# A hand-written stage order changed at three places, and the feed-forward transposes moved behind the per-layer projection

## The chip, the cores and the metric

The kernel runs on one core of a Trainium2 chip. The metric is the device time of one execution in microseconds (us). The engines are TensorE (PE, with PEld for its weight loads), VectorE (DVE), ScalarE (ACT), GpSimd (POOL) and SyncE (SP), which issues the DMA transfers.

## The reference

Two encoder layers are computed in float32 on x of 256 positions by 1024 channels. Cut to what matters here:

```python
h = rms_norm(x, g_mix)
proj = h @ w_in               # latents c_q, c_kv, k_r; d_q, d_k, d_v; s_q, s_k, s_v; gates
q = (rms_norm(c_q, g_q_lora) @ w_uq)     # latent attention "mla": rotary part from sin, cos
kv = (rms_norm(c_kv, g_kv_lora) @ w_ukv)
o_mla, o_diff, o_win = ...    # three attentions; the last two subtract slope * |distance|
merged = (gates[:, :, 0] * (o_mla @ w_branch[0]) + gates[:, :, 1] * (o_diff @ w_branch[1])
          + gates[:, :, 2] * (o_win @ w_branch[2]))
x = x + merged @ w_out
h = rms_norm(x, g_ffn)
x = x + (gelu(depthwise_conv(h @ w_ffn_gate)) * (h @ w_ffn_up)) @ w_ffn_down
e = rms_norm(pe @ w_ple_proj, g_ple)
return x + sigmoid(rms_norm(x, g_ple_in) @ w_ple_gate) * e
```

## The kernel before

Every product is made from three TensorE matmuls: each float32 operand is split into a high part (fp32r) and the low rest, and hi·hi, hi·lo and lo·hi are summed in PSUM. Weights come through the class `Stream` (`W`) in blocks of 128 x 1024 numbers: SP loads `raw` (L80), ACT copies it to `whi` (L91), and DVE subtracts to `wlo` (L92). Each of the three has four buffers; loads run four blocks ahead of use and splits two. Activations are turned by TensorE transposes (`TR`, L330) into PSUM banks and split there in the same way by `split` (L347: ACT at L349 or L352, DVE at L350 or L353). PSUM has four banks for transposes, scores and small outputs (`bank`) and four accumulators (`accbank`).

Of one layer, in the order of time: the projection "A" of the latents; then the mixers, whose stages stand in the string `ORDER` (L51 to L57), one word for a stage or for one weight block of a projection; then the output projection (`out1`), the per-layer projection of pe (`pp0`, `pp1`), the normalised x (`xn`), its transposes `ffnT`, and the feed-forward part in 11 steps of gate (`g`), up (`u`) and down blocks.

Words of `ORDER` that matter: `g01`, `g11`, `g20`, `g21` are units of gate projections (one weight block, 12 matmuls); `ukv0`, `uq0`, `uq1` the second latent projections; `Tmk0`, `Tmq0` transpose the normed keys (`uk00tok`, `uk01tok`) and queries (`uq00tok`, `uq01tok`) of the latent attention into banks `mk0b`, `mq0b`; `dq` is a projection for the differential attention; `dt3` transposes its last head (`od3` into `dot`) for the branch product `b10`; `ws1` are window scores (`w1s`), `wo0` and `wo3` window outputs (`w0o`, `w3o`); `b20` is the window's branch product.

What a key tile needs: POOL computes mean squares and inverse roots (`uk00ms`, `uk00ri` at L730 and L732, and the same for `uq`), and `positions_setup` (L269) makes angles, sine and cosine and the mask of distances once for both layers (DVE L277 to L310, ACT L304, POOL L311 and L313); POOL multiplies sine and cosine into rotary factors `rpq`, `rpk` (L256 to L259), DVE rotates the shared key (`kr`, `krr`, L424 to L427), POOL scales it (L550), and DVE writes both parts of `uk00tok` (L795, L796).

The Python order is only a first list. A scheduler of the framework orders each engine's instructions from it, by priorities; an engine then runs its own list strictly in order. `tc.high_priority(offset=HI)` moves work up in that choice. So the change of one place can move instructions of other engines.

Of the kernel before, what the change touches and what calls it, by code (L numbers as in the profile page):

```python
# [18 lines left out]
P = 128  # L19
D = 1024  # L20
S = 256
DEPTH = 2
KT = D // P
NT = S // P
# [11 lines left out]
HI = 400  # L36
# [3 lines left out]
R_CW, R_CB, R_MIX, R_FFN, R_PIN, R_QL, R_KL = 0, 66, 88, 96, 104, 112, 114  # L40
# [8 lines left out]


ORDER = """  # L51
g00 g00 cT g00 g00 g01 ukv0 uq0 g01 g01 Tmk0 g01 Tmq0 uq1 dq ukv1 dq dq dq ms0 Tmk1 ms1 dk Tmq1 mp0 dk dk mp1
dk Tdq dv ms2 mo0 ms3 dv mp2 dv Tdk mp3 dv sq ms4 mo1 ms5 sq sq mp4 sq mp5 ms6 skv mo2 mp6 skv ms7 mp7 ds0 mo3
b00 Tsq Tskv b00 dp0 ds1 b01 b01 do0 g10 ds2 g10 dp1 do1 g10 dt0 ds3 g10 dp2 g11 dt1 do2 dp3 ws0 g11 g11 do3
g11 dt2 wp0 dt3 b10 ws1 wo0 b10 ws2 b11 b11 g20 wp1 ws3 g20 wp2 g20 wo1 g20 wo2 wp3 wo3 b20 b20 g21 g21 g21
Tmg0 g21 b21 b21
"""  # L57

# [59 lines left out]
def kernel(ctx: ExitStack, tc: tile.TileContext, a: dict, out: bass.AP):  # L118
# [23 lines left out]
    def bank(name):  # L142
        return psm.tile([P, 512], F32, tag="ps", name=name)
# [8 lines left out]
    ident = const.tile([P, P], F32, name="ident")  # L152
# [173 lines left out]
    def MM(*args, **kw):  # L326
        last_pe[0] = nc.tensor.matmul(*args, **kw)  # L327

    def TR(o, i, idn):
        last_pe[0] = nc.tensor.transpose(o, i, idn)  # L330
# [16 lines left out]
    def split(hi, lo, src, scale=None):  # L347
        if scale is None:
            ih = nc.scalar.activation(hi, src, AF.Copy)  # L349
            il = nc.vector.tensor_tensor(lo, src, hi.bitcast(F32), op=ALU.subtract)  # L350
        else:
            ih = nc.scalar.activation(hi, src, AF.Copy, scale=scale)  # L352
            il = nc.vector.scalar_tensor_tensor(lo, src, scale, hi.bitcast(F32), op0=ALU.mult, op1=ALU.subtract)  # L353
        return ih, il
# [20 lines left out]
            res.append(ri)  # L375
        return res

    def transpose_half(src, h, hi, lo, gcol, name, scale=None, k_base=None):
        res = []
        for kp in range(2):  # L380
            b = bank(f"{name}T{h}{kp}")
            bv = b.rearrange("p (a n) -> p a n", a=2)
            for i in range(2):
                c = (kp * 2 + i) * P
                for t in range(NT):
                    TR(bv[:, i, t * P:(t + 1) * P], src[t][h][:, c:c + P], ident)
            k0 = (h * 4 if k_base is None else k_base) + kp * 2
            if gcol is None:
                res.append(split(hi[:, k0:k0 + 2, :], lo[:, k0:k0 + 2, :], bv, scale))
            else:  # L390
                for i in range(2):
                    res.append(split(hi[:, k0 + i, :], lo[:, k0 + i, :], bv[:, i, :], gcol(k0 + i)))
        return res

    def gemm(name, nk, n, lhs, evict, alloc=None):
# [99 lines left out]
    def layer(l):  # L495
        n_ = f"L{l}"
        g = G[l]
# [90 lines left out]
        gT = g["T"]  # L588
# [411 lines left out]
        def T_mg(h):  # L1000
            if not mlT:
                mlT["h"] = big.tile([P, KT, S], F32R, tag="big", name=n_ + "mTh")
                mlT["l"] = big.tile([P, KT, S], F32R, tag="big", name=n_ + "mTl")
            transpose_half(mg["m"], h, mlT["h"], mlT["l"], None, n_ + "mg", 0.5)
# [13 lines left out]
        for tok in PLAN:  # L1018
            op = tok[0]
            if op == "f":  # L1020
                c = tok[1]
# [38 lines left out]
        b = bank(n_ + "peT").rearrange("p (a n) -> p a n", a=2)  # L1060
# [10 lines left out]
        xn = [[xnt[:, t, h, :] for h in range(2)] for t in range(NT)]  # L1071
# [25 lines left out]
            yield from gemm(f"{n_}pp{h}", 2, 512, lhs_p, evict_e(h))  # L1097
        fT = [big.tile([P, KT // 2, 2, S], F32R, tag="big", name=f"{n_}fT{h}") for h in range(2)]
        for h in range(2):
            with tc.high_priority(offset=HI):  # L1100
                transpose_half(xn, h, fT[h][:, :, 0, :], fT[h][:, :, 1, :],
                               lambda k, h=h: gT[:, R_FFN + 4 * h + k:R_FFN + 4 * h + k + 1], n_ + "ffn", k_base=0)

        def finish_e():
            for f in late_e:
                f()
            for t in range(NT):
                s1 = small(1, f"{n_}se{t}")
                nc.gpsimd.tensor_tensor(s1, sse[t][:, 0:1], sse[t][:, 1:2], op=ALU.add)
                r = rsqrt_mean(s1, D, 1, f"{n_}e{t}")  # L1110
                rh = sm.tile([P, 1], F32, tag="reh", bufs=2, name=f"{n_}reh{t}")
                nc.gpsimd.tensor_scalar(rh, r, 0.5, None, op0=ALU.mult)
                nc.vector.tensor_scalar(e_t[:, t, :], e_t[:, t, :], rh, None, op0=ALU.mult)
# [9 lines left out]
        def down(s):  # L1123
            hh, hl = hid.pop(s)
            for i in range(2):
                wh, wl = W.get()
                first, last = s == 0 and i == 0, s == NF // 2 - 1 and i == 1
                th = [(t, h) for h in range(2) for t in range(NT)]
                if last:
                    steps = [(m, t, h) for t, h in th for m in range(3)]  # L1130
                else:
                    steps = [(m, t, h) for m in range(3) for t, h in th]
                for m, t, h in steps:
                    MM(dacc[t][h], (hl if m == 2 else hh)[:, i, t * P:(t + 1) * P],
                       (wl if m == 1 else wh)[:, 0, h * 512:(h + 1) * 512], start=first and m == 0, stop=last and m == 2)

        for s in range(NF // 2):
            pb = {}
            for nm in ("g", "u"):
                bs = [bank(f"{n_}{nm}{s}{i}") for i in range(2)]  # L1140
                ws = [W.get(), W.get()]
                for i in range(2):
                    c = slice(i * P, (i + 1) * P)
                    for k in range(KT):
                        wh, wl = ws[k // 4]
                        xp = fT[k // 4][:, k % 4]
                        MM(bs[i], wh[:, k % 4, c], xp.rearrange("p a n -> p (a n)"), start=k == 0, stop=False)
                        MM(bs[i][:, :S], wl[:, k % 4, c], xp[:, 0, :], start=False, stop=k == KT - 1)
                pb[nm] = tmp.tile([P, 2, S], F32, tag="p" if nm == "g" else "t512", bufs=5 if nm == "g" else 3, name=f"{n_}{nm}s{s}")
                for i in range(2):  # L1150
                    o = pb[nm][:, i, :]
                    nc.scalar.activation(o, bs[i][:, S:], AF.Copy)
                    nc.vector.tensor_tensor(o, bs[i][:, :S], o, op=ALU.add)  # L1153
                if s == 0 and nm == "g":
                    finish_e()
            c = tmp.tile([P, 2, S], F32, tag="p", name=f"{n_}c{s}")
            for i in range(2):
                ff = s * 2 + i

                def tap(j):  # L1160
                    r = R_CW + j * NF + ff
                    return gT[:, r:r + 1]

                nc.scalar.activation(c[:, i, :], pb["g"][:, i, :], AF.Identity, scale=tap(1), bias=gT[:, R_CB + ff:R_CB + ff + 1])  # L1164
                nc.vector.scalar_tensor_tensor(c[:, i, 1:S], pb["g"][:, i, 0:S - 1], tap(0), c[:, i, 1:S], op0=ALU.mult, op1=ALU.add)
                nc.vector.scalar_tensor_tensor(c[:, i, 0:S - 1], pb["g"][:, i, 1:S], tap(2), c[:, i, 0:S - 1], op0=ALU.mult, op1=ALU.add)
            cf = c.rearrange("p a n -> p (a n)")
            sq = tmp.tile([P, 512], F32, tag="t512", bufs=3, name=f"{n_}c2{s}")
            nc.scalar.activation(sq, cf, AF.Square)
            nc.vector.scalar_tensor_tensor(sq, sq, 1.0 / GELU_A, cf, op0=ALU.add, op1=ALU.mult)  # L1170
            th = tmp.tile([P, 512], F32, tag="p", name=f"{n_}th{s}")
            nc.scalar.activation(th, sq, AF.Tanh, scale=GELU_C * GELU_A)
            nc.vector.scalar_tensor_tensor(th, th, 1.0, cf, op0=ALU.add, op1=ALU.mult)
            hd = th
            nc.vector.tensor_tensor(hd, th, pb["u"].rearrange("p a n -> p (a n)"), op=ALU.mult)
            hh = ptp.tile([P, NT, S], F32R, tag="pthi", name=f"{n_}hh{s}")
            hl = ptp.tile([P, NT, S], F32R, tag="ptlo", name=f"{n_}hl{s}")
            split(hh, hl, hd.rearrange("p (a n) -> p a n", a=2), 0.5)
            hid[s] = (hh, hl)
            if s:  # L1180
                down(s - 1)
            yield
# [53 lines left out]
    for l in range(DEPTH):  # L1236
        for _ in layer(l):
            pass
# [24 lines left out]
```

## Time and profile before

| what | value |
|---|---|
| median of 3 runs | 931.65 us (931.29 to 932.65) |
| profiled execution | 933.81 us, of which its span is 931.9 us |
| mean granted TensorE clock | 0.997 |
| busy shares of the span | PE 98%, PEld 82%, DVE 78%, ACT 68%, POOL 13% |
| DMA | 155.9 MB, 167 GB/s mean |

The profiled execution is 2.16 us over the median, 0.23%; 1.9 us of it lie outside the span. A busy share counts overlapping matmuls once, and the granted clock of 1.00 is TensorE's 2.4 GHz, 0.50 its 1.2 GHz.

### The profile page before, as it was taken

How to read it: one execution, taken by the hardware profiler on the slowest of the kernel's cores; microseconds unless marked ns; L12 is line 12 of the kernel's file. 1: busy time of each engine (PE TensorE's matmuls, PEld its weight loads, DVE VectorE, ACT ScalarE, POOL GpSimd, SP SyncE). 2: the span in 40 equal slices, each digit the busy share in tenths (PEclk: the TensorE clock that was granted, in tenths of full speed). 3: DMA queues.
4: the chain of work that ended last, by engine and by line, in shares of the span. 5: the costliest groups of instructions: out<-in, count | busy, mean ns of one | idle time of the engine just before them, and what ended most of it. 6: DMA issues, size and time to landing. Idle time of an engine off the chain costs nothing.

```text
span 931.9 us, 13773 instructions
## 1 busy us (share of the span) xinstructions
PE 912.8 (98%) x4807; PEld 767.2 (82%) x4807; DVE 728.6 (78%) x1281; ACT 632.9 (68%) x1172; POOL 125.3 (13%) x239
## 2 busy tenths in 40 slices
PE   7999999999999999999999999999999999999997
PEld 6878887788888888888888888787887888888886
DVE  4788789887688877778777887989767877877784
ACT  5868877884567566566676788688755766656572
POOL 2834021000020000000134423000001100000010
PEclk9999999999999999999999999999999999999999
DMA  6656435355546556666556555344464565556642
GB/s 194 210 154 199 137 103 158 114 157 187 185 129 210 190 182 194 194 185 186 161 149 185 178 158 155 105 149 125 127 217 157 170 211 181 185 183 194 195 150 88
DMA packets 101706, 155.90 MB, mean 167 GB/s; under 512 B 7316, under 2 KB 58372, under 8 KB 101636
## 3 DMA queue, kind: packets, MB, share of 16 engines
q1 hardware_dynamic: 101636, 155.02, 53.7%
q8 instruction: 38, 0.62, 0.3%
q14 instruction: 32, 0.26, 0.1%
HBM read 153.95 MB, written 1.05 MB: 166 GB/s over the span
## 4 chain that ended last, share of the span: by engine, by line
PE 87%; POOL 3%; DVE 3%; ACT 2%; issue 2%; DMA 1%; SPq 1%; POOLq 0%; ACTq 0%; DVEq 0%
PE L1u L327 7%; PE L0u L327 7%; PE L1g L327 7%; PE L0g L327 7%; PE L1dn L327 6%; PE L0dn L327 6%; PE L0g20a L327 1%; PE L1g20a L327 1%; PE L0dva L327 1%; PE L1dva L327 1%; PE L1g00a L327 1%; PE L1dka L327 1%; PE L0dka L327 1%; PE L0pg0a L327 1%; PE L1g21a L327 1%
## 5 line engine op out<-in xcount | busy, mean ns | idle before, releaser
L92 DVE TENSOR_TENSOR wlo<-raw,whi 128x1024 fp32r<-128x1024 f32 (+3 forms) x292 | 350.5, 1205 | 90.6 <-ACT whi L91 89.7
L91 ACT ACTIVATE whi<-raw 128x1024 fp32r<-128x1024 f32 (+3 forms) x292 | 304.0, 1044 | 135.2 <-PE L0dn L327 13.1
L327 PE MATMUL L0u<-L0fT,whi 128*128 128x512 f32 x176 | 62.7, 398 | 0.0
L327 PE MATMUL L1u<-L1fT,whi 128*128 128x512 f32 x176 | 62.7, 398 | 0.0
L327 PE MATMUL L1g<-L1fT,whi 128*128 128x512 f32 x176 | 62.5, 398 | 0.0
L327 PE MATMUL L0g<-L0fT,whi 128*128 128x512 f32 x176 | 62.5, 398 | 0.0
L327 PE MATMUL L1u<-L1fT,wlo 128*128 128x256 f32 x176 | 49.4, 281 | 0.0
L327 PE MATMUL L0u<-L0fT,wlo 128*128 128x256 f32 x176 | 49.4, 281 | 0.0
L327 PE MATMUL L0g<-L0fT,wlo 128*128 128x256 f32 x176 | 49.2, 281 | 0.0
L327 PE MATMUL L1g<-L1fT,wlo 128*128 128x256 f32 x176 | 49.2, 281 | 0.0
L327 PEld LDWEIGHTS L1u<-L1fT,whi 128*128 128x128 f32 x176 | 33.1, 188 | 8.3
L327 PEld LDWEIGHTS L0u<-L0fT,whi 128*128 128x128 f32 x176 | 33.1, 188 | 8.2
L327 PEld LDWEIGHTS L1g<-L1fT,whi 128*128 128x128 f32 x176 | 33.0, 188 | 8.0
L327 PEld LDWEIGHTS L0g<-L0fT,whi 128*128 128x128 f32 x176 | 33.0, 188 | 8.0
L327 PEld LDWEIGHTS L1g<-L1fT,wlo 128*128 128x128 f32 x176 | 33.2, 189 | 0.5
L327 PEld LDWEIGHTS L0g<-L0fT,wlo 128*128 128x128 f32 x176 | 33.2, 189 | 0.5
L327 PEld LDWEIGHTS L0u<-L0fT,wlo 128*128 128x128 f32 x176 | 33.2, 189 | 0.0
L327 PEld LDWEIGHTS L1u<-L1fT,wlo 128*128 128x128 f32 x176 | 33.2, 189 | 0.0
L372 POOL TENSOR_SCALAR L1plem<-L1pless 128x1 f32<-128x1 f32 x2 | 1.5, 732 | 176.9 <-ACT L1plej L368 176.9
L372 POOL TENSOR_SCALAR L0plem<-L0pless 128x1 f32<-128x1 f32 x2 | 1.5, 728 | 176.9 <-ACT L0plej L368 176.9
L1164 ACT ACTIVATE L0c<-L0gs,gT 128x256 f32<-128x256 f32 x22 | 13.3, 603 | 17.3 <-DVE L0gs L1153 17.3
L1164 ACT ACTIVATE L1c<-L1gs,gT 128x256 f32<-128x256 f32 x22 | 13.3, 603 | 17.3 <-DVE L1gs L1153 17.3
(1732 smaller groups left out, 2564.7 us busy)
## 6 DMA issues: line engine op xcount, KB each, us to landing
raw<-in_w_in_dram SPq DMA_DIRECT2D x84, 512.0 KB
raw<-in_w_ffn_gate_dram SPq DMA_DIRECT2D x44, 512.0 KB
raw<-in_w_ffn_up_dram SPq DMA_DIRECT2D x44, 512.0 KB
raw<-in_w_ffn_down_dram SPq DMA_DIRECT2D x44, 512.0 KB
raw<-in_w_branch_dram SPq DMA_DIRECT2D x24, 512.0 KB
raw<-in_w_out_dram SPq DMA_DIRECT2D x16, 512.0 KB
raw<-in_w_ple_gate_dram SPq DMA_DIRECT2D x16, 512.0 KB
raw<-in_w_in_dram SPq DMA_DIRECT2D x8, 416.0 KB
```

The costliest lines, as they stand in the source:

```text
L91: ih = self.nc.scalar.activation(hi[:, :m], raw[:, :m], AF.Copy)
L92: il = self.nc.vector.tensor_tensor(lo[:, :m], raw[:, :m], hi[:, :m].bitcast(F32), op=ALU.subtract)
L327: last_pe[0] = nc.tensor.matmul(*args, **kw)
L372: nc.gpsimd.tensor_scalar(ms, ss[t][:, 0:1], ss[t][:, 1:2], EPS, op0=ALU.add, op1=ALU.add)
L1164: nc.scalar.activation(c[:, i, :], pb["g"][:, i, :], AF.Identity, scale=tap(1), bias=gT[:, R_CB + ff:R_CB + ff + 1])
```

## The change

Three groups of words in `ORDER` change places. `transpose_half` issues all its transposes first, alternates the banks from one 128-column block to the next where a gain is given per block (the transposes of normed x for the mixers, for the gate of the per-layer input and for the feed-forward part), and raises the priority only of the splits. In the feed-forward part the first gate step goes through its channel blocks in the outer loop, so that its two outputs alternate.

```diff
-g00 g00 cT g00 g00 g01 ukv0 uq0 g01 g01 Tmk0 g01 Tmq0 uq1 dq ukv1 dq dq dq ms0 Tmk1 ms1 dk Tmq1 mp0 dk dk mp1
+g00 g00 cT g00 g00 g01 ukv0 uq0 g01 g01 g01 Tmk0 uq1 Tmq0 dq ukv1 dq dq dq ms0 Tmk1 ms1 dk Tmq1 mp0 dk dk mp1
...
-g11 dt2 wp0 dt3 b10 ws1 wo0 b10 ws2 b11 b11 g20 wp1 ws3 g20 wp2 g20 wo1 g20 wo2 wp3 wo3 b20 b20 g21 g21 g21
+g11 dt2 wp0 b10 ws1 dt3 wo0 b10 ws2 b11 b11 g20 wp1 ws3 g20 wp2 g20 wo1 g20 wo2 wp3 b20 g21 wo3 b20 g21 g21
...
+        bs = [bank(f"{name}T{h}{e}").rearrange("p (a n) -> p a n", a=2) for e in range(banks)]
+        where = [(k // 2, k % 2) if gcol is None else (k % banks, k // banks) for k in range(4)]
+        for k, (e, i) in enumerate(where):
+            for t in range(NT):
+                TR(bs[e][:, i, t * P:(t + 1) * P], src[t][h][:, k * P:(k + 1) * P], ident)
+        with tc.high_priority(offset=prio):
...
+                for k, (e, i) in enumerate(where):
+                    res.append(split(hi[:, k0 + k, :], lo[:, k0 + k, :], bs[e][:, i, :], gcol(k0 + k)))
...
-            with tc.high_priority(offset=HI):
-                transpose_half(xn, h, fT[h][:, :, 0, :], fT[h][:, :, 1, :],
-                               lambda k, h=h: gT[:, R_FFN + 4 * h + k:R_FFN + 4 * h + k + 1], n_ + "ffn", k_base=0)
+            transpose_half(xn, h, fT[h][:, :, 0, :], fT[h][:, :, 1, :],
+                           lambda k, h=h: gT[:, R_FFN + 4 * h + k:R_FFN + 4 * h + k + 1], n_ + "ffn", k_base=0, prio=HI)
...
+                blocks = [(i, k) for i in range(2) for k in range(KT)]
+                if s == 0 and nm == "g":
+                    blocks.sort(key=lambda b: b[1])
```

What the scheduler makes of it is shown at three places. The first is DVE in layer 0, where the keys of the latent attention are finished; `kr`, `krr` are the shared rotary key, `uk..tok`, `uq..tok` the key and query tiles. Before:

```order
L761 TENSOR_REDUCE L0uq01ss<-L0uq01sq 128x4
L92 TENSOR_TENSOR wlo_671<-raw_596,whi_670 128x768
L795 TENSOR_TENSOR L0uk00tok<-L0ukv0a_557,L0uk00ri 128x4x64
L796 TENSOR_TENSOR L0uk00tok<-L0krr_420,L0uk00ri 128x4x32
L795 TENSOR_TENSOR L0uk01tok<-L0ukv0a_558,L0uk01ri 128x4x64
L796 TENSOR_TENSOR L0uk01tok<-L0krr_438,L0uk01ri 128x4x32
L766 TENSOR_TENSOR L0uq00tok<-L0uq0a_594,L0uq00ri 128x384
```

With the change (L795 and L796 of before are L798 and L799 there, L766 is L769):

```order
L769 TENSOR_TENSOR L0uq00tok<-L0uq0a_594,L0uq00ri 128x384
L92 TENSOR_TENSOR wlo_689<-raw_632,whi_688 128x1024
L305 TENSOR_SCALAR nsinT<-sinT 128x32
L92 TENSOR_TENSOR wlo_727<-raw_668,whi_726 128x512
L428 TENSOR_TENSOR L0kr_422<-L0araw_142,rpk_403 128x16
L428 TENSOR_TENSOR L0kr_440<-L0araw_143,rpk_403 128x16
L429 TENSOR_TENSOR L0kr_440<-L0araw_143,rpk_403 128x16
L430 TENSOR_TENSOR L0krr_420<-L0kr_421,L0kr_422 128x32
L769 TENSOR_TENSOR L0uq01tok<-L0uq0a_595,L0uq01ri 128x384
L430 TENSOR_TENSOR L0krr_438<-L0kr_439,L0kr_440 128x32
L799 TENSOR_TENSOR L0uk00tok<-L0krr_420,L0uk00ri 128x4x32
```

The whole of `positions_setup` and what hangs on it moved in layer 0: in the kernel before it stands at the start of the layer, between the first weight splits; now its DVE work comes after the split for `ukv0`, and the rotated key comes right ahead of `uk00tok`, behind two more weight splits. On POOL the rotary factors moved behind the inverse roots that they stood ahead of:

```order
L733 TENSOR_SCALAR L0uq01ms<-L0uq01ss,L0st 128x4
L735 TENSOR_TENSOR L0uq01ri<-L0uq01ms,mhalf 128x4
L259 TENSOR_TENSOR rpq_398<-sinT,gbc_292 128x2x16
L259 TENSOR_TENSOR rpk_403<-sinT,gbc_292 128x2x16
L256 TENSOR_TENSOR rpq_398<-cosT,gbc_292 128x2x16
L257 TENSOR_TENSOR rpq_398<-cosT,gbc_292 128x2x16
L256 TENSOR_TENSOR rpk_403<-cosT,gbc_292 128x2x16
L257 TENSOR_TENSOR rpk_403<-cosT,gbc_292 128x2x16
L258 TENSOR_TENSOR rpq_398<-nsinT,gbc_292 128x2x16
L258 TENSOR_TENSOR rpk_403<-nsinT,gbc_292 128x2x16
L553 TENSOR_SCALAR L0krr_420<-L0krr_420,L0st 128x32
L553 TENSOR_SCALAR L0krr_438<-L0krr_438,L0st 128x32
```

All eight factor products and both scalings of `krr` now wait for the last inverse root of the queries on POOL's list.

The second place is PE at the last head of the differential attention in layer 0 (the same in layer 1). Before:

```order
L327 MATMUL L0b10a_2244<-wlo_2158,L0od 128x512
L327 MATMUL L0b10a_2244<-whi_2157,L0od 128x512
L330 MATMUL L0dot_2238<-ident,L0od_2182 128x128 x2
L327 MATMUL L0b10a_2243<-whi_2157,L0od 128x512
L327 MATMUL L0b10a_2243<-wlo_2158,L0od 128x512
```

With the change:

```order
L327 MATMUL L0w1s_2258<-L0wkT,L0wqT 128x256
L327 MATMUL L0w1s_2259<-L0wkT,L0wqT 128x256
L330 MATMUL L0dot_2302<-ident,L0od_2182 128x128 x2
L327 MATMUL L0w0o<-L0w0h,L0wv 128x256
L327 MATMUL L0w0o<-L0w0l,L0wv 128x256
```

The two transposes moved behind six more matmuls of `b10` and the 12 of `w1s`.

The third place is ACT at the feed-forward transposes of layer 0 (the same in layer 1); `fT` is the split of the transposed `xn`, and `whi_3161` belongs to the fourth weight block of the first gate and up step. Before:

```order
L91 ACTIVATE whi_3155<-raw_3047 128x1024
L352 ACTIVATE L0fT_3085<-L0ffnT_3087,gT_323 128x256
L352 ACTIVATE L0fT_3086<-L0ffnT_3105,gT_323 128x256
L352 ACTIVATE L0fT_3085<-L0ffnT_3096,gT_323 128x256
L352 ACTIVATE L0fT_3086<-L0ffnT_3114,gT_323 128x256
L352 ACTIVATE L0fT_3085<-L0ffnT_3087,gT_323 128x256
L352 ACTIVATE L0fT_3086<-L0ffnT_3105,gT_323 128x256
L352 ACTIVATE L0fT_3085<-L0ffnT_3096,gT_323 128x256
L91 ACTIVATE whi_3161<-raw_3067 128x1024
L352 ACTIVATE L0fT_3086<-L0ffnT_3114,gT_323 128x256
```

With the change:

```order
L91 ACTIVATE whi_3155<-raw_3047 128x1024
L91 ACTIVATE whi_3161<-raw_3067 128x1024
L352 ACTIVATE L0fT_3085<-L0ffnT_3087,gT_323 128x256
L352 ACTIVATE L0fT_3085<-L0ffnT_3088,gT_323 128x256
L352 ACTIVATE L0fT_3086<-L0ffnT_3105,gT_323 128x256
L352 ACTIVATE L0fT_3086<-L0ffnT_3106,gT_323 128x256
L352 ACTIVATE L0fT_3085<-L0ffnT_3087,gT_323 128x256
L352 ACTIVATE L0fT_3085<-L0ffnT_3088,gT_323 128x256
```

The copy to `whi_3161` moved ahead of all eight splits, and DVE's list shows the same for its subtraction `wlo_3162`. On PE all 24 matmuls of `pp0` and `pp1` come first now, then the 16 transposes, then the first gate step; before, the transposes stood between the matmuls of `pp1`.

## Rows read from the trace of the kernel before

**Rows 1.** The page: busy time of each engine.

```profile
PE 912.8 (98%) x4807; PEld 767.2 (82%) x4807; DVE 728.6 (78%) x1281; ACT 632.9 (68%) x1172; POOL 125.3 (13%) x239
```

**Rows 2.** Waits of PE: waiting tile, releaser, us in total, times, longest.

```profile
PE L0mk0b L330 <- DVE L0uk00tok L796: 1.8, 1, 1.8
PE L1ffnT L330 <- DVE L1xn L1075: 1.4, 2, 0.9
PE L0ffnT L330 <- DVE L0xn L1075: 1.1, 2, 0.9
PE L0dot L330 <- DVE L0od L952: 0.6, 1, 0.6
PE L1dot L330 <- DVE L1od L952: 0.6, 1, 0.6
PE L0g00a L327 <- DVE wlo L92: 0.6, 1, 0.6
PE L0w3o L327 <- ACT L0w6h L349: 0.4, 1, 0.4
...
PE L1mk0b L330 <- DVE L1uk01tok L796: 0.2, 1, 0.2
```

**Rows 3.** Timeline of PE, start of layer 0: start, us, engine, line, tiles.

```profile
21.81 0.48 PE L327 MATMUL L0g00a<-whi,L0hTh 128*128 128x512 f32 x1
22.86 0.50 PE L327 MATMUL L0g00a<-wlo,L0hTh 128*128 128x512 f32 x1 [0.57 <-DVE wlo L92]
```

**Rows 4.** Timeline of PE, keys of the latent attention, layer 0.

```profile
45.77 0.39 PE L327 MATMUL L0g01a<-whi,L0hTl 128*128 128x512 f32 x1
47.95 0.28 PE L330 MATMUL L0mk0b<-ident,L0uk00tok 128*96 128x128 f32 x1 [1.80 <-DVE L0uk00tok L796]
...
53.35 0.39 PE L327 MATMUL L0g01a<-whi,L0hTl 128*128 128x512 f32 x1
53.58 0.27 PE L330 MATMUL L0mq0b<-ident,L0uq00tok 128*96 128x128 f32 x1
```

**Rows 5.** Windows there: us, busy PE, PEld, DVE, ACT, POOL, granted clock, DMA.

```profile
48.50:49.00 0.50, 0.50 (x5) 0.49 (x6) 0.50 (x2) 0.04 (x1) 0.20 (x1) 0.82 0.95 156
...
50.00:51.00 1.00, 1.00 (x4) 0.81 (x3) 1.00 (x4) 0.48 (x1) 0.00 (x0) 0.50 0.27 103
...
52.00:52.50 0.50, 0.50 (x3) 0.35 (x3) 0.50 (x2) 0.14 (x1) 0.00 (x0) 0.77 0.00 0
```

**Rows 6.** Timeline of POOL, layer 0, from rotary factors to the last inverse root.

```profile
27.51 0.25 POOL L259 TENSOR_TENSOR rpk<-sinT,gbc 128x32 f32<-128x32 f32 x1
...
34.91 1.15 POOL L550 TENSOR_SCALAR L0krr<-L0krr,L0st 128x32 f32<-128x32 f32 x1
...
47.62 1.08 POOL L732 TENSOR_TENSOR L0uq01ri<-L0uq01ms,mhalf 128x4 f32<-128x4 f32 x1
```

**Rows 7.** Timelines of DVE and PE: last split for the window output w0o, its start.

```profile
176.63 0.68 DVE L350 TENSOR_TENSOR L0w1l<-L0w1pt,L0w1h 128x512 fp32r<-128x512 f32 x1
...
178.51 0.39 PE L327 MATMUL L0w0o<-L0w0h,L0wv 128*128 128x256 f32 x1
```

**Rows 8.** Window of 1 us between the feed-forward transposes, layer 0.

```profile
257.00:258.00 1.00, 0.79 (x5) 0.56 (x5) 0.56 (x3) 0.20 (x1) 0.80 (x2) 1.00 0.94 257
```

**Rows 9.** Timelines of PE, ACT and DVE at the feed-forward start, layer 0.

```profile
262.19 0.39 PE L327 MATMUL L0g<-L0fT,whi 128*128 128x512 f32 x1
...
262.44 1.06 ACT L91 ACTIVATE whi<-raw 128x1024 fp32r<-128x1024 f32 x1 [0.52 <-ACT L0fT L352]
...
258.71 1.22 DVE L92 TENSOR_TENSOR wlo<-raw,whi 128x1024 fp32r<-128x1024 f32 x1
259.85 3.03 DVE L353 SCALAR_TENSOR_TENSOR L0fT<-L0ffnT,gT,L0fT 128x256 fp32r<-128x256 f32 x7
```

**Rows 10.** Timeline of PE there: end of out1, last transposes.

```profile
253.18 0.39 PE L327 MATMUL L0pp0a<-whi,L0pTh 128*128 128x512 f32 x1
...
258.46 1.60 PE L330 MATMUL L0ffnT<-ident,L0xn 128*128 128x128 f32 x12 [0.20 <-DVE L0xn L1075]
```

More of the change, by code (lines that the diff above doesn't have):

```diff
@@ L376, in x_stats, with transpose_half @@
         return res
-    def transpose_half(src, h, hi, lo, gcol, name, scale=None, k_base=None):
+    def transpose_half(src, h, hi, lo, gcol, name, scale=None, k_base=None, prio=0, banks=2):
         res = []
[L380 to L387, printed above, removed]
+        k0 = h * 4 if k_base is None else k_base
+        bs = [bank(f"{name}T{h}{e}").rearrange("p (a n) -> p a n", a=2) for e in range(banks)]
[4 more added lines that the diff above has]
+        with tc.high_priority(offset=prio):
             if gcol is None:
-                res.append(split(hi[:, k0:k0 + 2, :], lo[:, k0:k0 + 2, :], bv, scale))
-            else:
-                for i in range(2):
-                    res.append(split(hi[:, k0 + i, :], lo[:, k0 + i, :], bv[:, i, :], gcol(k0 + i)))
+                for e in range(2):
+                    k = k0 + 2 * e
+                    res.append(split(hi[:, k:k + 2, :], lo[:, k:k + 2, :], bs[e], scale))
+            else:
+                for k, (e, i) in enumerate(where):
+                    res.append(split(hi[:, k0 + k, :], lo[:, k0 + k, :], bs[e][:, i, :], gcol(k0 + k)))
         return res
@@ L1141, in layer @@
                 ws = [W.get(), W.get()]
-                for i in range(2):
-                    c = slice(i * P, (i + 1) * P)
[L1144 to L1148, printed above, removed]
+                blocks = [(i, k) for i in range(2) for k in range(KT)]
+                if s == 0 and nm == "g":
+                    blocks.sort(key=lambda b: b[1])
+                for i, k in blocks:
+                    wh, wl = ws[k // 4]
+                    xp = fT[k // 4][:, k % 4]
+                    c = slice(i * P, (i + 1) * P)
+                    MM(bs[i], wh[:, k % 4, c], xp.rearrange("p a n -> p (a n)"), start=k == 0, stop=False)
+                    MM(bs[i][:, :S], wl[:, k % 4, c], xp[:, 0, :], start=False, stop=k == KT - 1)
                 pb[nm] = tmp.tile([P, 2, S], F32, tag="p" if nm == "g" else "t512", bufs=5 if nm == "g" else 3, name=f"{n_}{nm}s{s}")
```

## The prediction

> **What bounds the kernel now.** I read the page first: TensorE is busy for 98% of the span [rows 1], so its work is the floor, and an order can only win or lose the few microseconds in which it waits. Next I read the waits of PE [rows 2]: leaving out the load of x, they are 1.8 us for the keys of layer 0 and 0.2 in layer 1, 1.1 and 1.4 for `xn`, 0.6 for `od3` in each layer, 0.6 for a weight split and 0.4 for `w3o`. Then I read the timeline around each wait, since a wait can cost more than its own length. At the keys of layer 0 the third unit of `g01` issues its last matmul at 45.77 and `mq0b` starts at 53.58 [rows 4]. One matmul later (0.23 us, from 53.35 to 53.58), at 46.00, leaves 7.58 us; eight transposes at 0.11 (1.60 us for 12 with the end of the last, rows 10) and 12 matmuls at 0.23 are 3.65 of them. So 3.9 us are lost, though the waits are only 2.0. The rest shows in the windows [rows 5]: the granted clock falls to 0.82 for half a microsecond, is 0.50 (1.2 GHz) from 49 to 52, and 0.77 in the next half. The missing clock adds up to 0.09 + 1.5 + 0.12 = 1.7 us. Before it fell, TensorE had stood still for 1.8 us and then issued only transposes.
>
> **The change, part by part.** Every stretch below is compared with its own rows; the total is set against the median.
>
> *Start of layer 0.* Between the first two matmuls of `g00` stand 1.05 us instead of 0.23 [rows 3], 0.57 of them a named wait for a weight split on DVE. In the kernel before, nine small DVE instructions of `positions_setup` stand ahead of that split; with the change they come later. Bounds: 0 if ACT's copy is the late one, -0.82 if all goes. I take -0.75.
>
> *Keys of layer 0.* The fourth `g01` unit now stands ahead of the transposes and was meant to cover the wait. PE would arrive at 46.00 - 0.75 + 2.76 = 48.0. But the keys come later as well. On POOL the last inverse root ended at 47.62 + 1.08 = 48.70 [rows 6]. It now loses the `krr` scaling of 1.15 us ahead of it, and a second, shorter one, and all before it may start 0.75 earlier: it ends between 46.0 and 47.6. Only then come the rotary factors, two of 0.25 before DVE may start [rows 6]. On DVE stand, from the first `kr` to `uk00tok`, two weight splits (1.22 as in rows 9, and half of that), four of the wider token products (under 0.68 as in rows 7; I take 0.4 to 0.5) and nine small ones of some 0.1 each; POOL's scaling of `krr` lies in between with 0.4 to 1.15. Together that is 4.8 to 5.4 us, estimated from these rows. The first key transpose can start between 50.8 and 53.0; I take 52.3, near the late end, because POOL's rows stretch when weight splits run beside them. The hole is 4.3 us (2.8 to 5.0). A hole longer than the one of 1.8 should cost the clock as that did, another 1.7. Lost: 6.0 instead of 3.9, so **+2.1** (+0.6 to +2.8). Moving `uq1` ahead of the query transposes costs nothing more: its 12 matmuls now cover the key splits.
>
> *Keys of layer 1.* No positions are made there; the unit covers the 0.2 [rows 2]: -0.2.
>
> *`dt3` behind half of `b10` and `ws1`.* The wait of 0.6 goes [rows 2], as `od3` is ready while `b10` and the scores still run. What is late next is the split `w1l`, which ends at 176.63 + 0.68 = 177.31, and `w0o` started at 178.51 [rows 7]: at most 1.2 can be won. The low half of `od3` now stands behind a weight split and four score instructions on DVE, so the second `b10` unit may wait 0.2. I take -1.0 a layer (-0.6 to -1.2), **-2.0** for two.
>
> *`wo3` behind `b20` and a `g21` unit.* The 0.4 for `w6h` goes [rows 2], and some interleaving with it. 12 matmuls of `g21` now stand between. The merged gate that the next transposes need still has 18 matmuls of cover. I take -0.6 a layer (-0.4 to -0.75), **-1.2** for two; layer 1 runs the same order.
>
> *Feed-forward start.* The 24 matmuls of `pp0` and `pp1` run from 253.18 to 258.6 [rows 10], then 16 transposes to 260.4. Neither waits any more, since `xn` is complete by then; that is what the reordering removes. But the copy `whi_3161` needs the last `pp1` matmul to free its buffer, and it now stands ahead of all splits on ACT: to 259.9 with its 1.06 [rows 9]. Its subtraction on DVE follows the split of 1.22 that starts at 258.71 and takes as long: to 261.1. Only then come the low halves, 3.03 / 7 = 0.43 each. The first gate matmul writes into the bank of the first transposes, and so waits for both blocks in it; the second of these is the fourth on DVE: 261.1 + 4 x 0.43 = 262.8, against 262.19 now [rows 9]. That is +0.65 a layer, **+1.3** for two. If only the first low half had to be awaited, it would be -0.7 a layer; that is the bound below. The alternating banks win nothing on this path, as ACT and DVE already keep the same pace. In the other places where they alternate (mixers, gate of the per-layer input) no wait of PE is in rows 2, and matmuls hide the splits; I cost them at nothing. If that cover were gone, the split of the first block would come two transposes, 0.2 us, later each time.
>
> *The clock there.* TensorE would stand still from 260.4 to 262.8, after 1.8 us with only transposes. Now it waits 0.9 and less there, and the clock stays 1.00 [rows 8]. The hole of 2.4 is longer than the 1.8 that took the clock at the keys [rows 4, 5]. Bounds: 0 and 1.7 a layer. I take 1.7, as the nearest row is that hole: **+3.4** for two.
>
> The Trainium skill, "TensorE: Matmul & The Clock Gate", section on how HAM oscillation bites in real kernels, blames idle gaps between bursts of matmuls and names a length up to which the clock should stay; the new hole is shorter than that, so by the page the sum would lack the 3.4. The trace disagrees: the hole of 1.8, shorter still, was followed by 0.50.
>
> **The sum.** -0.75 + 2.1 - 0.2 - 2.0 - 1.2 + 1.3 = -0.75; with the clock +3.4, **+2.65**. From the median, 931.65 + 2.65 = **934.3**. The profiled execution was 2.16 over the median, and would by the same sum come to 936.5.
>
> **The rivals.**
>
> *The clock holds at one or both feed-forward starts.* The fall needs a hole at an unlucky moment; the smaller holes of rows 8 pass. One layer: 932.6. Both: 930.9. For it speaks that the mean clock holds through all else, against it that 1.8 us was enough.
>
> *The keys come in time (the other side: faster).* If the rotated key is ready before TensorE finishes `g01`, the mechanism is the one the new order is made for: the 3.9 us vanish instead of becoming 6.0, so 934.3 - 6.0 = 928.3, or 924.9 with the clock kept too. It decides at 48.0: uk00tok complete by then. For it: POOL loses the scalings, and ACT is free of two table changes early on. Against it: eight factor products and two scalings now stand behind the roots, and the roots ended at 48.70.
>
> *The won waits come back.* If what `dt3` and `wo3` win is taken back by the next late split, softmax or weight block, the 3.2 us are missing: 937.5. DVE at 78% speaks for a little of that, the absence of other waits in rows 2 against.
>
> *The change does not do what it says.* The order shows that it does at all places, so it has no chance of its own.
>
> **How the numbers follow.** About 0.2% or 1.9 us is what a measurement can tell from no change: faster is below 929.8, slower above 933.5. Forecast 0.42, clock kept at one or both 0.32, keys in time 0.18, waits come back 0.08. Each case has an uncertainty of some 1.5 us from its terms. Faster: the 0.18, and 0.06 of the second case: 0.24. Slower: two thirds of the forecast's 0.42, the 0.08 and 0.02 of the second case: 0.38. The rest, 0.38, is the same. The likeliest case's own range is 932.5 to 936.2. For 8 in 10 it has to reach down to keys in time with the clock lost (928.3) and up to the forecast with the late ends of its bounds; 928.5 to 936.5.
>
> **What would show it.** Right: the wait of `mk0b` in layer 0 is 3 to 5 us and the clock 0.50 behind it; the waits of `dot` and `w3o` are gone; the first gate matmul waits 2 to 2.5 us for `fT` in each layer; the 0.57 at `g00` is gone. Wrong: `mk0b` without a wait; the splits of `fT` under way before the copy of the fourth weight block ends; a clock of 1.00 behind the feed-forward hole; new waits in `b10`, `b20` or at the transposes of the merged gate.

## The result: slower, and the profile after

The changed kernel takes 937.76 us (median of 7 executions, 935.51 to 940.01); the kernel before, on the same chip, 931.29 us (7, 930.59 to 934.57). The ratio is 1.0062, 95% interval 1.0045 to 1.0078. The predicted 934.3 had the sign and was 3.5 us short; its range ended at 936.5.

The profiled execution took 937.54 us with a span of 935.8: 3.73 us over the profiled execution of before. The page says that TensorE's work is still the floor, as in [rows 1]:

```profile
PE 913.6 (98%) x4807; PEld 769.7 (82%) x4807; DVE 728.0 (78%) x1281; ACT 632.0 (68%) x1172; POOL 121.0 (13%) x239
```

What changed stands in the waits of PE (waiting tile, releaser, us in total, times, longest), to be read against [rows 2]:

```profile
PE L0mk0b L330 <- DVE L0uk00tok L799: 4.5, 1, 4.5
...
PE L1g L327 <- DVE L1fT L353: 2.4, 1, 2.4
PE L0g L327 <- DVE L0fT L353: 2.4, 1, 2.4
...
PE L0dqb L330 <- DVE L0tok L627: 1.3, 1, 1.3
PE L0g00a L327 <- DVE wlo L92: 0.7, 1, 0.7
```

`dot`, `w3o`, `ffnT` and the keys of layer 1 wait no more. The keys of layer 0 wait 4.5 us instead of 1.8, each gate of the feed-forward part 2.4, and there is a wait that no term of the prediction has: `dqb`, the queries of the differential attention.

**The keys of layer 0.** Timeline of PE (start, us, engine, line, tiles, in brackets the wait): the last `g01` matmul, the first key transpose, the second matmul of `uq1`, the first matmul of `dqa`:

```profile
47.74 0.39 PE L327 MATMUL L0g01a<-whi,L0hTl 128*128 128x512 f32 x1
...
52.62 0.64 PE L330 MATMUL L0mk0b<-ident,L0uk00tok 128*96 128x128 f32 x2 [4.49 <-DVE L0uk00tok L799]
...
54.51 0.67 PE L327 MATMUL L0uq1a<-wlo,L0cTh 128*128 128x384 f32 x1
...
58.17 0.57 PE L327 MATMUL L0dqa<-whi,L0hTh 128*128 128x512 f32 x1
```

Windows there (us, busy PE, PEld, DVE, ACT, POOL, granted clock, DMA): the clock is 1.2 GHz for some six microseconds, three in [rows 5].

```profile
51.00:52.00 1.00, 0.00 (x0) 0.00 (x0) 0.79 (x5) 0.00 (x0) 0.42 (x2) 0.85 0.77 100
...
52.50:57.50 5.00, 4.88 (x18) 4.81 (x19) 4.64 (x13) 1.81 (x3) 0.33 (x1) 0.50 0.58 190
58.00:59.00 1.00, 1.00 (x5) 0.82 (x4) 0.00 (x0) 0.53 (x2) 0.92 (x2) 0.74 0.57 213
```

Why the keys are late shows on POOL: the rotary factors stand behind the last inverse root and then wait for `nsinT` of DVE. In [rows 6] `rpk` was made at 27.51.

```profile
45.94 1.03 POOL L735 TENSOR_TENSOR L0uq01ri<-L0uq01ms,mhalf 128x4 f32<-128x4 f32 x1
...
47.15 0.26 POOL L259 TENSOR_TENSOR rpk<-sinT,gbc 128x32 f32<-128x32 f32 x1
...
50.34 0.63 POOL L258 TENSOR_TENSOR rpq<-nsinT,gbc 128x32 f32<-128x32 f32 x1 [2.10 <-DVE nsinT L305]
...
51.76 0.39 POOL L553 TENSOR_SCALAR L0krr<-L0krr,L0st 128x32 f32<-128x32 f32 x1 [0.58 <-DVE L0krr L430]
```

And on DVE `nsinT` stands between two weight splits, as the listing ahead of the prediction had it:

```profile
48.96 1.21 DVE L92 TENSOR_TENSOR wlo<-raw,whi 128x1024 fp32r<-128x1024 f32 x1
50.09 0.17 DVE L305 TENSOR_SCALAR nsinT<-sinT 128x32 f32<-128x32 f32 x1
50.18 0.68 DVE L92 TENSOR_TENSOR wlo<-raw,whi 128x512 fp32r<-128x512 f32 x1
```

**The new wait, `dqb`.** Timeline of DVE, first of the kernel before, then of the changed one: the sum of squares of the second query half, and its scaling, for which `dqb` waits.

```profile
75.29 0.67 DVE L611 TENSOR_REDUCE L0dq1ss<-L0dq1sq 128x8 f32<-128x512 f32 x1
...
79.85 0.69 DVE L624 TENSOR_TENSOR L0tok<-L0tok,L0dq1tot 128x512 f32<-128x512 f32 x1 [0.75 <-POOL L0dq1tot L618]
```

```profile
86.42 0.68 DVE L614 TENSOR_REDUCE L0dq1ss<-L0dq1sq 128x8 f32<-128x512 f32 x1
...
89.57 0.69 DVE L627 TENSOR_TENSOR L0tok<-L0tok,L0dq1tot 128x512 f32<-128x512 f32 x1 [1.89 <-POOL L0dq1tot L621]
```

It begins on ACT with the square `dq1sq`, first before and then changed. It runs nine microseconds later now, behind two softmax tiles, four splits and two weight copies.

```profile
72.85 0.63 ACT L609 ACTIVATE L0dq1sq<-L0tok 128x512 f32<-128x512 f32 x1
...
81.82 0.62 ACT L612 ACTIVATE L0dq1sq<-L0tok 128x512 f32<-128x512 f32 x1
```

**The feed-forward start, layer 0.** Timelines of PE, ACT and DVE, to be read against [rows 9]:

```profile
261.67 1.93 PE L330 MATMUL L0ffnT<-ident,L0xn 128*128 128x128 f32 x16
261.91 1.06 ACT L91 ACTIVATE whi<-raw 128x1024 fp32r<-128x1024 f32 x1 [1.66 <-PE L0pp1a L327]
261.99 2.35 DVE L92 TENSOR_TENSOR wlo<-raw,whi 128x1024 fp32r<-128x1024 f32 x2
...
264.26 2.83 DVE L353 SCALAR_TENSOR_TENSOR L0fT<-L0ffnT,gT,L0fT 128x256 fp32r<-128x256 f32 x7
...
265.97 0.50 PE L327 MATMUL L0g<-L0fT,whi 128*128 128x512 f32 x1 [2.37 <-DVE L0fT L353]
```

The transposes run without a wait; then DVE subtracts two weight blocks in 2.35 us before its first half of `fT`, and TensorE stands still for 2.37. Windows behind the hole, layer 0 and then layer 1:

```profile
266.00:268.00 2.00, 2.00 (x8) 1.72 (x9) 2.00 (x6) 0.78 (x3) 0.00 (x0) 0.69 0.80 257
268.00:270.00 2.00, 2.00 (x9) 1.71 (x8) 1.87 (x4) 0.41 (x2) 0.00 (x0) 0.50 0.08 27
270.00:272.00 2.00, 2.00 (x12) 1.78 (x12) 0.36 (x1) 1.45 (x3) 0.00 (x0) 0.96 0.03 8
...
722.00:726.00 4.00, 3.85 (x22) 3.37 (x23) 4.00 (x9) 2.19 (x5) 0.00 (x0) 1.00 0.47 153
```

In layer 0 the clock that is missing adds up to 0.62 + 1.0 + 0.08 = 1.7 us; in layer 1, where the hole ends at 722.1, it costs no clock.

### The profile page after: what moved, and what is told of

Its sections match the earlier page's. It is cut to its first block, busy times and chain, and to the rows that moved or that the text cites. A ratio compares the mean times of both kernels' runs of the same rounds, so it can differ in the third digit from the quotient of the medians.

```text
span 935.8 us, 13766 instructions
## 1 busy us (share of the span) xinstructions
PE 913.6 (98%) x4807; PEld 769.7 (82%) x4807; DVE 728.0 (78%) x1281; ACT 632.0 (68%) x1172; POOL 121.0 (13%) x239
## 4 chain that ended last, share of the span: by engine, by line
PE 89%; DVE 3%; POOL 3%; issue 2%; DMA 1%; ACT 1%; SPq 0%; POOLq 0%; DVEq 0%; ACTq 0%
PE L0g L327 7%; PE L1g L327 7%; PE L1u L327 7%; PE L0u L327 7%; PE L1dn L327 6%; PE L0dn L327 6%; DVE wlo L92 1%; PE L0g11a L327 1%; PE L1g11a L327 1%; PE L1g20a L327 1%; PE L0g20a L327 1%; PE L0dqa L327 1%; PE L1dva L327 1%; PE L1dka L327 1%; PE L0pg0a L327 1%
## 5 line engine op out<-in xcount | busy, mean ns | idle before, releaser
L372 POOL TENSOR_SCALAR L1plem<-L1pless 128x1 f32<-128x1 f32 x2 | 2.5, 1257 | 178.0 <-ACT L1plej L368 178.0
L372 POOL TENSOR_SCALAR L0plem<-L0pless 128x1 f32<-128x1 f32 x2 | 2.5, 1256 | 178.0 <-ACT L0plej L368 178.0
```

What stands on the lines that cost most here:

```text
L372: nc.gpsimd.tensor_scalar(ms, ss[t][:, 0:1], ss[t][:, 1:2], EPS, op0=ALU.add, op1=ALU.add)
```

## The experiments

Two theories stood after this reading. The first: the keys and `dqb` are late because the scheduler put other work ahead of theirs, and what made it do so is the new way of issuing the very first transposes of x, with its alternating banks, not the words of `ORDER`, which are good. The rival: the words of `ORDER` are the cause, or the won waits come back. A third question was the feed-forward start: whether its 2.4 us come from the weight block ahead of the splits, or from the late transposes themselves. "Before" beside a run is the kernel before on the same chip.

### One part undone or done alone

**First transposes as before** (the changed kernel, the function of before for the first transposes of layer 0):

```diff
-                    transpose_half(x, h, hTh, hTl, lambda k: gm[:, k:k + 1], n_ + "mix")
+                    transpose_old(x, h, hTh, hTl, lambda k: gm[:, k:k + 1], n_ + "mix")
```

> The changed kernel, but the first transposes of layer 0 (of x) use the banks one after the other as before; all else as changed. Built, positions_setup and the rotary factors stand where they stood before, and so do the reductions for the differential queries. Theory A (the late keys come from the moved positions): PE finds the keys of layer 0 ready after g01 (no wait at mk0b over 0.3 us), no wait at dqb, and clock 1.00 there; the 7.3 us lost at the keys and the 1.5 at dqb go: 929 to 931 us. Rival B (the moved words of the order string make the keys late): the wait of 4.5 us stays, 936 to 938 us.

931.91 us (12 executions, 930.45 to 933.94; before 931.70), ratio 1.0002 (0.9994 to 1.0011). The waits of `mk0b` and `dqb` are gone: this one edit holds, by the ratios, 0.6%, as much as the whole loss. It came out 0.9 over the expected band. Its profile has a wait of 1.3 at `mq0b` that the changed kernel lacks, and still the two holes of 2.4 at the feed-forward starts, of which the second lost the clock this time (0.80 from 714 to 718, 0.77 from 718 to 722) and the first kept it.

**Feed-forward start as before** (the changed kernel, `transpose_old` under `high_priority(offset=HI)` there, and no sorting of `blocks`):

> The changed kernel, but the feed-forward transposes and the first gate step as before; all else as changed. Theory A: the two holes of 2.4 us before the first gate matmul go, and with them a clock loss of 1.7 us in one or two layers; the keys stay late: 933 to 935.5 us. Rival C (the hole replaces stalls of the same size, and the clock falls elsewhere): 937 to 938 us.

935.45 us (5, 935.15 to 936.08; before 931.70), ratio 1.0040 (1.0028 to 1.0052), as expected. The transposes wait 1.4 a layer again, and by the medians 2.3 us come back in all. In the profiles 0.9 of the gain lie at the keys, where this execution lost less clock (1.7 instead of 3.0). The waits of `mk0b` (4.5) and `dqb` (1.3) stay, so the feed-forward part is not their cause.

**The words of `ORDER` alone** (the kernel before with the first two pairs of lines of the diff, nothing else):

> The kernel before with only the three groups of words in the order string changed. Theory A: the waits of the keys (layer 0 and 1), dot and w3o are gone, the 3.9 us lost at the keys of layer 0 come back, the two other places give 1.1 us a layer: 925 to 927 us. Rival B (the moved words are what costs): 931 us or more, with a wait at mk0b or new waits at w2s, b20 of the size of what is won.

927.79 us (5, 927.61 to 928.58; before 931.70), ratio 0.9957 (0.9945 to 0.9970): faster than both kernels, by 3.9 us, 0.8 over the expected band. This fells the rival. Timeline of PE: the key transposes follow `g01` without a wait. The window behind them keeps the full clock. Of the waits of PE, those of `dot`, `w3o` and `mk0b` are gone, and `mq0b` has one of 0.4.

```profile
48.82 0.39 PE L327 MATMUL L0g01a<-whi,L0hTl 128*128 128x512 f32 x1
49.05 0.27 PE L330 MATMUL L0mk0b<-ident,L0uk00tok 128*96 128x128 f32 x1
```

```profile
49.00:53.00 4.00, 3.58 (x25) 3.19 (x23) 4.00 (x11) 3.75 (x7) 0.00 (x0) 1.00 0.42 103
```

**The first transposes alone** (the kernel before with the new `transpose_half`, called `transpose_new`, at this one place):

```diff
-                    transpose_half(x, h, hTh, hTl, lambda k: gm[:, k:k + 1], n_ + "mix")
+                    transpose_new(x, h, hTh, hTl, lambda k: gm[:, k:k + 1], n_ + "mix")
```

> The kernel before, with the new order and alternating banks in the first transposes of x in layer 0 alone; everything else, the ORDER words too, as before. My theory now: this small part by itself moves positions_setup on DVE and the rotary factors on POOL behind the inverse roots, and dq1ss behind other work. TensorE would reach the keys at 46 as before, and the keys would be ready at about 52.5 as in the changed kernel: a wait of mk0b of 5.5 to 6.5 us where it was 1.8, clock 0.50 behind it, and a new wait of about 1.3 at dqb: slower than before by 4.5 to 7 us, 936 to 939. Rival, that the moves come from the ORDER words or from the other transposes: nothing changes, 930.5 to 932.5, mk0b waits 1.8.

940.66 us (4, 939.97 to 941.03; before 932.07), ratio 1.0088 (1.0075 to 1.0102): 8.6 us slower, more than the whole change and 1.7 over the expected band. Waits of PE and the last root and first factor on POOL:

```profile
PE L0mk0b L330 <- DVE L0uk00tok L816: 4.5, 1, 4.5
...
PE L0dqb L330 <- DVE L0tok L644: 2.6, 1, 2.6
```

```profile
46.55 1.03 POOL L752 TENSOR_TENSOR L0uq01ri<-L0uq01ms,mhalf 128x4 f32<-128x4 f32 x1
...
47.77 0.25 POOL L259 TENSOR_TENSOR rpk<-sinT,gbc 128x32 f32<-128x32 f32 x1
```

The factors stand behind the roots though not one word of `ORDER` has changed. The wait of `mk0b` is shorter and that of `dqb` longer than expected, and the hole at `dqb` now costs clock as well (0.76 and 0.82 over the next two stretches of 4 us: 1.7 us), which the expectation lacked. So the new function at this one place is shown to be the cause. That it is its alternating banks, and not the order of its transposes, is not shown here: no version with the new function and unalternated banks was run.

### What in them does it

**Positions raised** (the changed kernel with one line more):

```diff
         if l == 0:
-            positions_setup()
+            with tc.high_priority(offset=HI):
+                positions_setup()
```

> The changed kernel with one addition: positions_setup is given a raised priority, so that its work stands early again on DVE and POOL and the rotary factors come ahead of the inverse roots; the alternating banks of the first transposes stay, and dq1ss stays late. If the late positions alone make the keys late: mk0b waits less than 1 us, no clock of 0.50 behind it, dqb still waits about 1.3, both gates of the feed-forward part wait 2.4: 5 us under the changed kernel, 931.5 to 934. Rival, that the splits of the first transposes or another part of DVE's list make the keys late: mk0b still waits over 3 us, 936 to 938.5.

936.17 us (5, 935.13 to 936.96; before 932.07), ratio 1.0038 (1.0024 to 1.0051): by its time in the rival's band, by its waits the theory's: `mk0b` does not wait, the clock keeps 1.00 there, `dqb` waits 1.3, the gates 2.4 each. From the start of `g01` to the first scores (`L0m0s`) TensorE is 4.7 us quicker than in the changed kernel (3.42 lost against the kernel before there, here 1.31 won). The time did not come, for two reasons: the load of x came 1.4 us later in this execution than in that of the changed kernel (`L0Aa` at 11.16 and 9.79), and the raised work has its price at another place. Waits of PE:

```profile
PE L0g00a L328 <- DVE wlo L92: 2.4, 2, 1.7
```

Timeline of DVE there:

```profile
30.58 0.30 DVE L280 CAST pos_row<-pos_row_i 128x256 f32<-128x256 int32 x1 [2.28 <-DMA pos_row_i<-in_positions_dram]
...
32.91 1.22 DVE L92 TENSOR_TENSOR wlo<-raw,whi 128x1024 fp32r<-128x1024 f32 x1
```

DVE stops 2.28 us for the row of positions from memory, and the next weight split stands behind it. In the kernel before, the splits of that moment stand ahead of `pos_row` (32.11 there). So late positions make the keys late; to raise all of them is no cure.

**The fourth weight block behind the splits** (the changed kernel; `tr` holds the splits that `transpose_half` returns, and the scheduler must put the copy and subtraction of the named block behind the last of them):

```diff
+        W.behind[W.ns + 1] = tr[1][3]
```

> The changed kernel with one dependency more in the feed-forward part: the copy and subtraction of the fourth weight block must follow the last split of the transposed x. Theory A (this block ahead of the splits makes the hole): the first gate matmul waits 1.0 to 1.5 us instead of 2.4, its clock stays 1.00 more often: 933 to 936 us. Rival D (the hole is the time of transposes and splits themselves): the wait stays above 2 us, 937 to 938 us.

935.02 us (5, 934.67 to 935.38; before 931.70), ratio 1.0035 (1.0023 to 1.0047), as expected. `L0g` waits 1.4, `L1g` 1.5, and the clock is 1.00 behind both. The weight block ahead of the splits is thus 0.9 to 1.0 us of each hole, near the 1.2 that the prediction gave its subtraction. Left are 1.4 and 1.5, where `ffnT` waited 1.1 and 1.4 in the kernel before [rows 2]. Whether late transposes then win anything, the last runs below show.

### The gains apart, and the best version

**The key words alone:**

> The kernel before with only the first group of ORDER words (the fourth unit of g01 ahead of the key transposes, uq1 ahead of the query transposes). If the key words bring most of what the ORDER words bring, the wait of mk0b goes and with it the fall of the clock: 2 to 3.5 us under before, 928.2 to 929.7, and the words of dt3 and wo3 bring the rest of 0.4 to 1.9. Rival, that dt3 and wo3 bring most (1.0 to 1.6 a layer): 930 to 931.3.

931.04 us (11, 930.56 to 932.27; before 932.07), ratio 0.9990 (0.9981 to 0.9999). 1.0 us, which is the rival's band: `dt3` and `wo3` bring most. The wait of `mk0b` is gone, and a new one has come, one stage on. Waits of PE and the DVE work behind which it stands:

```profile
PE L0mq0b L330 <- DVE L0mkT L353: 1.4, 1, 1.4
```

```profile
52.56 0.68 DVE L92 TENSOR_TENSOR wlo<-raw,whi 128x512 fp32r<-128x512 f32 x1
53.16 1.40 DVE L353 SCALAR_TENSOR_TENSOR L0mkT<-L0mk0b,gT,L0mkT 96x512 fp32r<-96x512 f32 x2
```

**The words of `dt3` and `wo3` alone:**

> The kernel before with only the second and third group of ORDER words (dt3 behind half of b10 and ws1, wo3 behind b20 and a g21 unit). From the run with all ORDER words, where the stretch from the second differential scores to the transposes of the merged gate is 1.1 to 1.2 us a layer shorter than before: 2.3 under before in all, about 929.5, and with the key words alone (1.0 under) the sum of the two is 3.3, near the 3.9 of all words. The forecast on record had -1.6 a layer, 928.8. Rival, that the won waits come back: 931 to 932.

929.52 us (7, 929.10 to 931.16; before 932.23), ratio 0.9973 (0.9961 to 0.9984): 2.7 us, near the 2.3 expected. The waits of `dot` and `w3o` do not come back.

**All words, and the versions beside them.** Three runs on one chip, before 932.23. The first repeats the words alone. The second adds the late feed-forward transposes with the fourth block behind; an earlier run of the same version stands under its own expectation. The third has the words and the alternating banks, but only in layer 1 and at the gate of the per-layer input.

> The kernel before with all ORDER words, once more, to stand beside the next two on the same chip: 927.6 to 928.4.

> The changed kernel with the first transposes of x as before and with the fourth weight block of each feed-forward start placed behind the last split of fT. Against the run with the ORDER words alone (927.8) it adds the late feed-forward transposes without the two copies ahead of their splits, and the alternating banks of layer 1. Theory: with the block behind, the late transposes are worth a little, as the runs so far suggest (0.2 to 0.4 us a layer): 926.5 to 928, L0g and L1g wait about 1.4, clock 1.00. Rival, that the late transposes cost time however the blocks stand, because TensorE has nothing to do while they are split: 928.5 to 931.

> The version with the ORDER words, the old first transposes and the fourth weight block of each feed-forward start behind the splits of fT, beside the ORDER words alone. By the stages of the two traces the feed-forward starts gain 0.3 to 0.6 us a layer: 0.6 to 1.2 under the run with the ORDER words alone. Rival, that the late transposes only change the place of the 1.4 us: within 0.3 of it.

> The ORDER words with the alternating banks in the mixers' transposes of layer 1 and in the gate of the per-layer input, but with the first transposes of layer 0 and the feed-forward start as before. The forecast costed alternating banks at those places at nothing: within 0.3 us of the ORDER words alone. Rival, that they move other work as the first transposes did: a new wait in the trace and over 1 us more.

| version | us | ratio to before |
|---|---|---|
| words alone | 929.00 (928.63 to 929.24) | 0.9963 (0.9950 to 0.9975) |
| words, ffn behind, first run (before 932.07) | 927.73 (927.42 to 928.09) | 0.9951 (0.9938 to 0.9963) |
| words, ffn behind, beside | 927.75 (927.50 to 928.79) | 0.9952 (0.9939 to 0.9964) |
| words, later alternation | 929.17 (928.53 to 929.83) | 0.9965 (0.9953 to 0.9978) |

The words alone came out 0.6 us above the expected band. The late transposes are worth 1.25 us beside them once the weight block is behind, just over the 0.6 to 1.2 expected, with holes of 1.4 and no clock lost; so they do more than move the old wait to another place. The alternation at the later places changes nothing that can be seen. The best version is the change without its first transposes and with one line for the fourth block: 4.5 us under the kernel before, 10 under the changed one.

## Why the prediction was wrong, step by step

Starts of the same matmuls in the two PE timelines, changed minus before, give each stage its share. The load of x came 0.92 us earlier in this execution.

| step | predicted | measured | from the starts of |
|---|---|---|---|
| `g00` | -0.75 | +0.2 | `L0Aa` -0.92, `L0g01a` -0.75 |
| keys, layer 0 | +2.1 | +3.4 | to `L0m0s` +2.67 |
| queries `dqb` | none | +1.5 | to `L0m2s` +4.22 |
| `dt3`, `wo3`, layer 0 | -1.6 | -1.2 | to `L0mgT` +3.05 |
| feed-forward start, layer 0 | +2.35 | +2.3 | to `L0u` +5.36 |
| keys, layer 1 | -0.2 | -0.3 | `L1ukv0a` to `L1m0s` +4.73 |
| `dt3`, `wo3`, layer 1 | -1.6 | -1.1 | to `L1mgT` +3.60 |
| feed-forward start, layer 1 | +2.35 | +0.5 | to `L1u` +4.11 |

Behind each feed-forward start another 0.3 is won. With these and the -0.92 the measured shares make +3.8, and the profiled times differ by 3.73.

**Two steps failed.** The one that by its size accounts for the miss of 3.5 us is the term of the keys of layer 0, "Lost: 6.0 instead of 3.9, so +2.1". The changed kernel lost 7.5 there, 4.5 of wait and 3.0 of clock, and the 3.9 held for the profiled execution: most executions of before lost about 2.0, judging by their clocks (below, under the base). That would make the term +5.5, 3.4 over the forecast. The other misses of the table, the load of x and the 0.3 behind each feed-forward start cancel to about 0.2, which is luck.

The step that failed in its mechanism is "In the other places where they alternate (mixers, gate of the per-layer input) ... I cost them at nothing"; the first transposes of layer 0 are among the mixers', and the new function at that one place costs 8.6 us by itself. The listing had shown the moved positions, and I put the consequence down to the change as a whole; I looked neither for which edit moved them nor for what else it had moved. The square of `dq1` stood on ACT's list, nine microseconds later, for +1.5. I had read the lists of DVE and POOL around the keys only.

**Keys of layer 0.** Start and hole were right: 52.62 against 52.3, a wait of 4.5 against a hole of 4.3. The term of the clock was mis-sized: the 1.7 seen behind the hole of 1.8 [rows 5], where from 52.6 on 3.0 are missing (half of 5.4 us at 1.2 GHz, and 0.26 from 58 to 59). It is not a fixed price either. The run with the feed-forward start as before has the same hole of 4.5 (it ends at 53.1), and its windows miss 1.7:

```profile
52.00:56.00 4.00, 2.88 (x13) 2.61 (x14) 3.77 (x16) 1.32 (x2) 0.90 (x2) 0.72 0.71 255
56.00:60.00 4.00, 4.00 (x23) 3.69 (x22) 2.29 (x5) 2.34 (x4) 1.34 (x2) 0.86 0.47 135
```

**The base.** The terms were taken against the profiled execution of before, and the sum was added to the median. But the 1.7 us of clock at the keys belong to that execution, not to the kernel: of 43 executions of before beside the experiments, 39 have a mean clock of 0.998 or more and take 930.6 to 932.8 us, and four have 0.997 and take 934.1 to 934.3; none lies between. The profiled one, at 933.81 and 0.997, was of the rare kind. The text even gave its 2.16 us over the median, and put 1.9 of them down to time outside the span, which is there in every execution. Judging by these clocks and times, most executions of before lost the 2.0 of the waits at the keys and not 3.9; no trace of such an execution shows it. That would be most of why the medians lie 6.1 (against 931.65) to 6.5 us apart where the profiles differ by 3.7, and part of why the key words alone won only 1.0.

**`g00`.** The nine small instructions went and the wait stayed (0.57 in [rows 3], now 0.67). The split on DVE, first before and then changed, starts 0.76 earlier and now waits for ACT's copy; TensorE arrived 0.85 earlier, because of the load of x, so nothing was won. In the three other profiles in which the positions are late and the load of x is not early (first transposes alone, feed-forward start as before, fourth block behind) the stage gains 0.2, 0.35 and 0.04. ACT's copy was the late one, near the end of the bound that I did not take.

```profile
21.59 1.22 DVE L92 TENSOR_TENSOR wlo<-raw,whi 128x1024 fp32r<-128x1024 f32 x1
...
20.83 1.23 DVE L92 TENSOR_TENSOR wlo<-raw,whi 128x1024 fp32r<-128x1024 f32 x1 [5.45 <-ACT whi L91]
```

TensorE in the changed kernel:

```profile
20.96 0.48 PE L327 MATMUL L0g00a<-whi,L0hTh 128*128 128x512 f32 x1
22.11 0.50 PE L327 MATMUL L0g00a<-wlo,L0hTh 128*128 128x512 f32 x1 [0.67 <-DVE wlo L92]
```

**`dt3` and `wo3`.** Right in mechanism, -2.3 instead of -3.2 for two layers; the 2.7 of the run with these words alone agrees.

**Feed-forward start.** Right in layer 0 to 0.1 us, the clock's 1.7 included. In layer 1 the hole of 2.4 kept the clock, so half of the rival with the kept clock came true. The late block of weights as a cause of the hole is confirmed by the run that put it behind: 0.9 to 1.0 of the 2.4 us went.

**The rivals.** "The keys come in time" decides at 48.0, and `uk00tok` came at 52.5; with the old first transposes the mechanism is real, as the words alone show. "The won waits come back" reached nearly the measured time, 937.5, but for another reason: those waits stayed won.

**The clock** behind a hole differs from execution to execution. Holes of 1.4 to 1.5 us at the feed-forward start (six, in the three profiles with the block behind) kept it, holes of 4.5 and 5.6 at the keys (four profiles) lost it, and holes of about 2.4 did both within one execution; that of 1.8 in [rows 4] lost it. The time of an execution goes with its mean clock: executions of the changed kernel with a mean clock of 0.998 take 935.5 and 935.9, those with 0.991 take 938.5 and 940.0. The Trainium skill, "TensorE: Matmul & The Clock Gate", section on how HAM oscillation bites in real kernels, would have all holes of 2.4 harmless; the windows above show one at 0.50.

What stays open is why the scheduler answers to the new function in the first transposes by moving positions and `dq1` back: the runs show that the new function at that place makes it do so, not by which part of the function or by which of its numbers.

## What to carry to other kernels

A scheduler that orders engines from a list of priorities can answer a tiny edit at the start of a program with a new order far away; where a listing shows a large move, find the edit that makes it by applying each part alone, and follow all lists that it touches, ACT's small squares too. Before adding a sum to a median, ask whether the profiled execution has a loss that the median has not. And judge the parts of a change singly: here one part, worth 8.6 us of loss by itself, hid the 3.9 that another had won.

## What the runs showed that was not expected

A new way to issue 16 transposes at the start cost 8.6 us through the order of other engines. Raising the work that had become late moved DVE's stop for a transfer (2.28 us) ahead of a weight split, and 2.2 of the 4.7 us won were lost again in the stage of `g00`. The clock behind a hole of 2.4 us differs from layer to layer and from run to run: 0.69 and 0.50 in layer 0 and 1.00 in layer 1 of the changed kernel, the other way round with the first transposes as before.
